# A hybrid decoder layer on one core: rotary row swap by small transfers, attention scores on 64 rows per map, and three convolution taps per channel group on TensorE

## The chip, the cores and the metric

The kernel runs on one core of one Trainium2 chip. The metric is the device time of one execution in microseconds (us), the median over runs. Engines are named as in the profile: PE is TensorE (matmuls; PEld are its weight loads), DVE is VectorE, ACT is ScalarE, POOL is GpSimd, SP is the engine whose queue issues most transfers.

## The reference, cut to what matters

One layer over 512 positions of width 1024. After an RMS norm one projection feeds two groups: a causal depthwise convolution with 31 taps over 512 channels, and differential attention with 4 heads, each with two softmax maps of head size 64. Their outputs are joined, projected back and added. Then follow an expert retrieval over 16384 single-neuron experts, and a gated embedding. The change touches only the first two groups:

```python
def rope(x, pos):                      # x: ..., 64 values per map
    ...
    x1, x2 = x[..., :half], x[..., half:]
    return jnp.concatenate([x1 * cos - x2 * sin, x2 * cos + x1 * sin], axis=-1)

def diff_attention(q, k, v, lam, subln_g, lambda_init):
    qf = rope(q.astype(jnp.float32), pos) * (d ** -0.5)
    kf = rope(k.astype(jnp.float32), pos)
    ...                                # per block of 128 queries:
        s = jnp.einsum('bhcqd,bhckd->bhcqk', qblk, kf)      # c: the two maps
        s = jnp.where(mask, s, -jnp.inf)
        pr = jax.nn.softmax(s, axis=-1)
        a = pr[:, :, 0] - lam * pr[:, :, 1]
        return jnp.einsum('bhqk,bhkd->bhqd', a, vf)
    ...

def conv_module(cv, cg, w, b, ln_g, ln_b):
    u = cv * jax.nn.sigmoid(cg)
    y = lax.conv_general_dilated(u, w[:, None, :], (1,), [(CONV_KERNEL - 1, 0)], ...) + b   # one filter per channel
    return jax.nn.silu(layer_norm(y, ln_g, ln_b))
```

## The kernel before, in words

Channels lie on the 128 partitions and the 512 positions along the free dimension in the whole front part. A projection tile (`proj`, line 144) is 128 output channels by 512 positions: the weight tile is loaded (512 KB), split into a high and a low part in a rounded float type (`split`, line 62: ACT makes the high part, DVE the low one), and multiplied in three products for each of 8 slices of the contraction, 24 matmuls in all (`mm3`, line 66, so lines 67 to 69 in the profile). Plain f32 matmuls, such as the scores, appear in the trace as two matmul instructions each.

The order of the front part in the program is: the eight projections of the convolution (loop at line 182: gate, value, product `u`), the value projections of the attention (line 216), then `qk(h)` for heads 0 and 1, and the loop at line 332, which runs over the 16 units (head, block of 128 queries). In it `att_scores` (line 248) computes the two maps of a unit, adds the causal mask by one more matmul (`identb`, `maskb`), takes the negated maximum on DVE and the exponential on ACT. `att_mix` follows two units later, `att_value` three, and `qk(h + 2)` stands behind the last unit of head `h`. Embedding products (`embed`, line 321) fill the middle. `sub_norm` and `head_out` finish a head; for all but the last head the inverse square root runs on POOL and DVE waits for it. Then come the loading and splitting of the eight tiles of the output weight (line 355), the convolution's taps (line 363), its layer norm (line 369), and the output projection (`outp`, line 402).

That is the program's order only. A planner writes each engine's queue: it takes the instructions by priority as their inputs become ready in its own estimate, and the order so found is fixed. So the taps, which stand behind the attention in the program, run on DVE from the moment `u` exists, in whatever places are free. Each engine then works its queue strictly in that order and waits where an input is late. SP's queue of transfers is such a queue too.

`qk(h)` rotates q and k: the 128 rows of a tile are two maps of 64, and the rotation needs row p next to row p XOR 32. Before, that swap is a matmul with a permutation matrix (`perm`, lines 232 and 233), of which DVE reads the result from PSUM (line 235). DVE then multiplies the rows by cos (line 236, in place) and adds. For k the sum goes into `kr` (line 238). For q it goes into `qz` (line 242), which holds each map in its own copy, with the other map's 64 rows zero; POOL writes these zeros at the start (lines 155 to 157). The scores (line 253) therefore contract 128 rows, of which 64 are zero.

The convolution keeps its output in `cy`: ACT writes the first tap and the bias (line 364), and DVE adds the other 30 taps of each of the four channel groups, one instruction of 128x512 each (line 366).

Of the kernel before, what the change touches and what calls it, by code (L numbers as in the profile page):

```python
# [10 lines left out]
F32 = mybir.dt.float32  # L11
# [5 lines left out]
AF = mybir.ActivationFunctionType  # L17
OP = mybir.AluOpType
# [3 lines left out]
S, D = 512, 1024  # L22
NT = S // 128
KT = D // 128
H, HD = 4, 64
TAPS = 31
NH, NK, TOPK = 8, 128, 16
HC = 2 * NH
NA = 3
# [25 lines left out]
def hymba_layer(ctx: ExitStack, tc: tile.TileContext, I, out):  # L55
    nc = tc.nc
    V, A, P, T = nc.vector, nc.scalar, nc.gpsimd, nc.tensor

    def load(dst, src):
        nc.sync.dma_start(dst, src)  # L60
# [28 lines left out]
    def cload(name, shape, src, pool=None):  # L89
        t = (pool or att).tile(shape, F32, name=name)  # L90
        load(t, src)
        return t
# [4 lines left out]
    def bank():  # L97
        return psf.tile([128, 512], F32, name="bank")

    def bank2():  # L100
        return psf.tile([128, 512], F32, name="bank2", bufs=2)
# [4 lines left out]
    cy = mid.tile([128, 4, S], F32, name="cy")  # L106
    att = tc.alloc_tile_pool(name="att", bufs=1, side="right")
    inp = tc.alloc_tile_pool(name="inp", bufs=1)
# [35 lines left out]
    def proj(i, w=None):  # L144
        hi, lo = w or weight(I["w_in"][i], [128, KT, 128])
        ps = bank()
        for k in range(KT):
            mm3(ps, hi[:, k], lo[:, k], aH[:, k], aL[:, k], k == 0, k == KT - 1)
        return ps

    PADW = TAPS - 1
    u = mid.tile([128, 4, PADW + S], F32, name="u")
    V.memset(u[:, :, 0:PADW], 0.0)
    qz = att.tile([128, H, 2, S], F32, name="qz")
    for h in range(H):
        P.memset(qz[64:128, h, 0], 0.0)
        P.memset(qz[0:64, h, 1], 0.0)
    kr = att.tile([128, H, S], F32, name="kr")
    vn = att.tile([128, NT, S], F32, name="vn")
    pgs = proj(12 + 4, (hi0, lo0))  # L160
    ident = cload("ident", [128, 128], I["ident"], const)
    iota = cload("iota", [128, 128], I["iota"].to_broadcast([128, 128]), const)
    convw = cload("convw", [128, 4, TAPS], I["convw"], mid)
    convb = cload("convb", [128, 4], I["convb"], mid)
# [12 lines left out]
    for t in range(NT):  # L177
        rb = inp.tile([128, 128], F32, name="rb", bufs=2)
        A.activation(rb, ones, AF.Copy, scale=rn[:, t:t + 1])
        T.matmul(rp[:, t * 128:t * 128 + 128], rb, ident, start=True, stop=True)  # L180
    A.activation(r1, rp, AF.Copy)
    for ct in range(4):
        pg = pgs if ct == 0 else proj(12 + 4 + ct)
        sg = inp.tile([128, S], F32, name="sg", bufs=2)
        V.tensor_tensor(sg, pg, r1, op=OP.mult)
        A.activation(sg, sg, AF.Sigmoid)
        pv = proj(12 + ct)
        cvr = inp.tile([128, S], F32, name="cvr", bufs=2)
        V.tensor_tensor(cvr, pv, r1, op=OP.mult)
        V.tensor_tensor(u[:, ct, PADW:], cvr, sg, op=OP.mult)  # L190

    perm = cload("perm", [128, 128], I["perm"])
    cos = cload("cos", [128, S], I["cos"])
    sin = cload("sin", [128, S], I["sin"])
    cmask = cload("cmask", [128, 128], I["cmask"])
# [4 lines left out]
    maskb = att.tile([128, 128], BF16, name="maskb")  # L200
    identb = att.tile([128, 128], BF16, name="identb")
# [15 lines left out]
    for k2 in range(KT // 2):  # L217
        hi, lo = weight(I["w_v"][k2], [128, 2, S])
        for j in range(2):
            k = 2 * k2 + j  # L220
            for t in range(NT):
                sl = slice(t * 128, t * 128 + 128)
# [4 lines left out]
    def qk(h):  # L227
        for isk in range(2):
            ps = proj(4 * isk + h)
            raw = inp.tile([128, S], F32, name="qraw", bufs=2)  # L230
            A.activation(raw, ps, AF.Copy, scale=1.0 if isk else HD ** -0.5)
            pp = bank2()
            T.matmul(pp, perm, raw, start=True, stop=True)
            rot = inp.tile([128, S], F32, name="rot", bufs=2)
            V.tensor_tensor(rot, pp, sin, op=OP.mult)
            V.tensor_tensor(raw, raw, cos, op=OP.mult)
            if isk:
                V.tensor_tensor(kr[:, h], raw, rot, op=OP.add)
            else:
                for c in range(2):  # L240
                    sl = slice(c * HD, c * HD + HD)
                    V.tensor_tensor(qz[sl, h, c], raw[sl], rot[sl], op=OP.add)


    zz = att.tile([128, H, NT, 5], F32, name="zz")
# [1 line left out]

    def att_scores(h, t):
        W = (t + 1) * 128
        pr = []  # L250
        for c in range(2):
            ps = bank()
            T.matmul(ps[:, :W], qz[:, h, c, t * 128:W], kr[:, h, :W], start=True, stop=False)
            T.matmul(ps[:, t * 128:W], identb, maskb, start=False, stop=True)
            nm = att.tile([128, 1], F32, name="nm", bufs=8)
            V.tensor_reduce(nm, ps[:, :W], axis=AX.X, op=OP.max, negate=True)
            p = att.tile([128, S], F32, name="p%d" % c, bufs=MIX + 2)
            A.activation(p[:, :W], ps[:, :W], AF.Exp, bias=nm, accum_out=zz[:, h, t, c:c + 1])
            pr.append(p)
        un[h, t] = pr  # L260
# [67 lines left out]

    units = [(h, t) for h in range(H) for t in range(NT)]
    qk(0)  # L330
    qk(1)
    for i in range(len(units) + MIX + 1):
        if i < len(units):
            h, t = units[i]
            att_scores(h, t)
            if t == NT - 1 and h + 2 < H:
                qk(h + 2)
        if 0 <= i - MIX < len(units):
            att_mix(*units[i - MIX])
        if 0 <= i - MIX - 1:  # L340
            h, t = units[i - MIX - 1]
            att_value(h, t)
            if t == 2 and h > 0:
                head_out(h - 1)
        if i == EMB:
            embed_load()
        if 0 <= i - EMB - 1 < 2 * NT:
            embed(*divmod(i - EMB - 1, 2))
# [6 lines left out]
    for k in range(KT):  # L355
        raw = wop.tile([128, D], F32, name="woraw", bufs=2)
# [4 lines left out]


    for ct in range(4):
        A.activation(cy[:, ct], u[:, ct, 0:S], AF.Identity, scale=convw[:, ct, 0:1], bias=convb[:, ct:ct + 1])
        for j in range(1, TAPS):
            V.scalar_tensor_tensor(cy[:, ct], u[:, ct, j:j + S], convw[:, ct, j:j + 1], cy[:, ct], op0=OP.mult, op1=OP.add)


# [28 lines left out]
    op = tc.alloc_tile_pool(name="op", bufs=2, reuse_waits="tile")  # L397
# [71 lines left out]
    def rbank():  # L469
        return psr.tile([128, 512], F32, name="rbank")  # L470
# [170 lines left out]
    for h in range(NH):  # L641
        for c in range(2):
            raw = wqp.tile([128, KT, 128], F32, name="qraw", bufs=3)
# [5 lines left out]
            ps = rbank()  # L649
# [157 lines left out]
    for c in range(NK):  # L807
# [25 lines left out]
        if NU <= c < NU + 2 * KT and (c - NU) % 2 == 0:  # L833
            k = (c - NU) // 2
            raw = tw.tile([128, D], F32, name="et")
# [45 lines left out]
def _arrays(a):  # L881
# [9 lines left out]
        "subg": c(a["subln_g"][0][:, None]),  # L891
        "convw": c(a["conv_w"][0].T.reshape(4, 128, TAPS).transpose(1, 0, 2)),
        "convb": c(a["conv_b"][0].reshape(4, 128).T),
# [41 lines left out]
```

## Time and profile before

| | |
|---|---|
| median of 3 runs | 1573.29 us (1571.17 to 1575.72) |
| profiled execution | 1571.18 us, of which the span from first to last instruction is 1569.4 us |
| PE, DVE, ACT, POOL busy over the span | 96%, 80%, 46%, 30% |
| granted TensorE clock, mean over the span | 0.987 of full speed |

The shares over the whole span are a mean over stages with different limits. From about 300 us on the kernel streams the experts' weights through TensorE, with DMA busy; the front part, which is changed, is the first 250 us. In the rows, a time at the head of a line is the start in us from the start of the span, and the number behind it is the time from the start of the first to the end of the last instruction that the line merges; "x4" is their number. In brackets stands how long the engine was idle before it and who ended that. TensorE's matmuls overlap, so the distance between two starts, not the duration, tells what a matmul takes in a stream.

### The profile page before, as it was taken

The numbers are of one execution on the slowest core, as the hardware profiler recorded it, in microseconds if no ns is written. First come the engines' busy times: TensorE is split into PE (matmuls) and PEld (weight loads), VectorE is DVE, ScalarE is ACT, GpSimd is POOL, SyncE is SP. The second block draws the span as 40 slices with busy tenths as digits, with TensorE's granted clock in tenths as the row PEclk, the third lists the DMA queues.
The fourth block names the chain that finished last, engine by engine and source line by source line (L and its number), as shares of the span: only waits on it lengthen the run. The fifth ranks groups of instructions, "written<-read, shape, count | busy, mean of one in ns | idle before, by whom it ended". The sixth has DMA issues, their size and how long they took to land. (4 is left out here: it accounts for less than half of the span.)

```text
span 1569.4 us, 22408 instructions
## 1 busy us (share of the span) xinstructions
PE 1512.0 (96%) x7945; PEld 1319.3 (84%) x7945; DVE 1250.5 (80%) x2415; ACT 720.7 (46%) x1133; POOL 469.6 (30%) x324
## 2 busy tenths in 40 slices
PE   8999898999999999999999999999999999998997
PEld 6867566889999988999999888888888888886886
DVE  4999863799999999988885578878778787768756
ACT  5433664223347755776666433333333333234433
POOL 1000103331223344344443234444344443432000
PEclk9999998999999999999999999999999999999999
DMA  7220245311779999999999998899999898989712
GB/s 240 94 81 28 74 161 211 104 59 41 255 213 332 333 340 332 345 388 392 356 360 370 334 369 322 325 338 335 336 330 334 301 327 304 323 327 327 243 40 81
DMA packets 147296, 408.27 MB, mean 260 GB/s; under 512 B 14576, under 2 KB 65776, under 8 KB 145648
## 3 DMA queue, kind: packets, MB, share of 16 engines
q1 hardware_dynamic: 109744, 270.51, 48.9%
q0 software_dynamic: 36864, 134.23, 22.7%
q10 hardware_dynamic: 576, 2.10, 0.3%
q8 instruction: 62, 1.02, 0.3%
q14 instruction: 50, 0.41, 0.1%
HBM read 355.48 MB, written 51.31 MB: 259 GB/s over the span
## 5 line engine op out<-in xcount | busy, mean ns | idle before, releaser
L582 POOL DMA_INDIRECT row<-in_v,bidx x128 | 213.1, 1665 | 299.5 <-DVE acc L593 283.0
L582 POOL DMA_INDIRECT row<-in_u,bidx x128 | 194.6, 1521 | 349.2 <-DVE row L585 304.5
L69 PE MATMUL ups<-mTH,ulo 128*128 128x384 f32 x760 | 256.9, 338 | 3.7 <-DVE ulo L607 3.6
L67 PE MATMUL ups<-mTH,uhi 128*128 128x384 f32 x760 | 258.0, 339 | 0.0
L68 PE MATMUL ups<-mTL,uhi 128*128 128x384 f32 x760 | 256.3, 337 | 0.0
L746 PE MATMUL y<-vlo,hH 128*128 128x512 f32 x768 | 239.4, 393 | 7.0 <-DVE vlo L64 7.0
L746 PE MATMUL y<-vhi,hH 128*128 128x512 f32 x768 | 238.7, 392 | 3.6 <-ACT vhi L63 3.6
L606 ACT ACTIVATE uhi<-uraw 128x1024 fp32r<-128x1024 f32 x128 | 135.2, 1060 | 229.7 <-PE ups L68 157.4
L746 PE MATMUL y<-vhi,hL 128*128 128x512 f32 x768 | 238.4, 392 | 0.0
L63 ACT ACTIVATE hH<-hf 128x384 fp32r<-128x384 f32 x128 | 67.2, 525 | 298.9 <-PE y L746 227.4
L607 DVE TENSOR_TENSOR ulo<-uraw,uhi 128x1024 fp32r<-128x1024 f32 x124 | 150.4, 1218 | 46.6 <-ACT uhi L606 43.3
L746 PEld LDWEIGHTS y<-vlo,hH 128*128 128x128 f32 x768 | 144.8, 189 | 40.1 <-DVE vlo L64 9.7
L746 PEld LDWEIGHTS y<-vhi,hH 128*128 128x128 f32 x768 | 144.3, 189 | 33.7 <-ACT vhi L63 5.1
L585 DVE SCALAR_TENSOR_TENSOR row<-row,mB 128x1024 f32<-128x1024 f32 x128 | 152.3, 1221 | 25.2 <-DMA row<-in_u,bidx 25.1
L746 PEld LDWEIGHTS y<-vhi,hL 128*128 128x128 f32 x768 | 145.4, 189 | 30.6
L593 DVE SCALAR_TENSOR_TENSOR acc<-row,bh,acc 128x1024 f32<-128x1024 f32 x127 | 162.3, 1278 | 0.0
L64 DVE TENSOR_TENSOR hL<-hf,hH 128x384 fp32r<-128x384 f32 x128 | 71.2, 556 | 113.9 <-ACT hH L63 113.9
L64 DVE TENSOR_TENSOR vlo<-vraw,vhi 128x1024 fp32r<-128x1024 f32 x128 | 156.0, 1219 | 3.4 <-ACT vhi L63 3.2
L69 PEld LDWEIGHTS ups<-mTH,ulo 128*128 128x128 f32 x760 | 142.6, 188 | 5.4 <-DVE ulo L607 5.3
L67 PEld LDWEIGHTS ups<-mTH,uhi 128*128 128x128 f32 x760 | 142.7, 188 | 1.1 <-ACT av L613 0.3
L68 PEld LDWEIGHTS ups<-mTL,uhi 128*128 128x128 f32 x760 | 142.7, 188 | 1.0
L63 ACT ACTIVATE vhi<-vraw 128x1024 fp32r<-128x1024 f32 x128 | 135.6, 1059 | 8.7 <-DMA vraw<-in_v 8.4
(280 smaller groups left out, 2629.1 us busy)
## 6 DMA issues: line engine op xcount, KB each, us to landing
uraw<-in_ut SPq DMA_DIRECT2D x128, 512.0 KB, 6.3
vraw<-in_v SPq DMA_DIRECT2D x128, 512.0 KB, 5.0
g_spill<-stage SPq DMA_DIRECT2D x12, 2048.0 KB, 10.2
gt<-g_spill SPq DMA_DIRECT2D x16, 1536.0 KB, 11.3
a_spill<-av SPq DMA_DIRECT2D x101, 192.0 KB, 6.7
ga<-a_spill SPq DMA_DIRECT2D x101, 192.0 KB, 6.4
qraw<-in_wq SPq DMA_DIRECT2D x16, 512.0 KB, 3.6
wraw<-in_w_in SPq DMA_DIRECT2D x15, 512.0 KB, 3.7
```

The costliest lines, as they stand in the source:

```text
L63: A.activation(hi, src, AF.Copy)
L64: V.tensor_tensor(lo, src, f32(hi), op=OP.subtract)
L67: T.matmul(ps, wh, xh, start=first, stop=False)
L68: T.matmul(ps, wh, xl, start=False, stop=False)
L69: T.matmul(ps, wl, xh, start=False, stop=last)
L582: P.indirect_dma_start(out=row, out_offset=None, in_=I["u"] if i < 128 else I["v"], in_offset=bass.IndirectOffsetOnAxis(ap=bidx[:, j:j + 1 ...
L585: tc.keep_in_program_order(V.scalar_tensor_tensor(row, row, 1.0, mB, op0=OP.mult, op1=OP.mult, accum_out=ba[:, j:j + 1]))
L593: tc.keep_in_program_order(V.scalar_tensor_tensor(acc, row, bh[:, j:j + 1], acc, op0=OP.mult, op1=OP.add))
L606: A.activation(hi, raw, AF.Copy)
L607: (P if c in first[:POOLED] else V).tensor_tensor(lo, raw, f32(hi), op=OP.subtract)
L746: T.matmul(y[t][n], w[:, sl], x[:, n * 512:n * 512 + 512], start=c == 0 and w is hH and x is hi, stop=c == NK - 1 and l)
```

## The change

It has three parts. The rotary swap becomes four transfers of 32 rows from the tile `raw` to a new tile `swap`, on SP's queue; the product with cos, which overwrites `raw`, comes after them. q is kept once (`qr`, 128 rows with both maps), one addition each for q and k, and each map's scores contract its own 64 rows; both maps' scores are issued before the two mask matmuls. And the first three taps of each channel group are matmuls of `u` with a diagonal matrix that ACT makes from `ident`, summed in PSUM, from where ACT writes them with the bias to `cy`; DVE adds the other 28.

```diff
+PTAPS = 3
...
-    qz = att.tile([128, H, 2, S], F32, name="qz")
-    for h in range(H):
-        P.memset(qz[64:128, h, 0], 0.0)
-        P.memset(qz[0:64, h, 1], 0.0)
+    qr = att.tile([128, H, S], F32, name="qr")
...
+    def first_taps(ct):
+        ps = bank()
+        for j in range(PTAPS):
+            dg = inp.tile([128, 128], F32, name="rb", bufs=2)
+            A.activation(dg, ident, AF.Copy, scale=convw[:, ct, j:j + 1])
+            T.matmul(ps, dg, u[:, ct, j:j + S], start=j == 0, stop=j == PTAPS - 1)
+        A.activation(cy[:, ct], ps, AF.Identity, bias=convb[:, ct:ct + 1])
+
     for ct in range(4):
...
         V.tensor_tensor(u[:, ct, PADW:], cvr, sg, op=OP.mult)
-
-    perm = cload("perm", [128, 128], I["perm"])
+        if ct:
+            first_taps(ct - 1)
+    first_taps(3)
+
...
-            pp = bank2()
-            T.matmul(pp, perm, raw, start=True, stop=True)
+            swap = inp.tile([128, S], F32, name="swap", bufs=2)
+            for p in range(0, 128, 32):
+                load(swap[p:p + 32], raw[p ^ 32:(p ^ 32) + 32])
+            V.tensor_tensor(raw, raw, cos, op=OP.mult)
             rot = inp.tile([128, S], F32, name="rot", bufs=2)
-            V.tensor_tensor(rot, pp, sin, op=OP.mult)
-            V.tensor_tensor(raw, raw, cos, op=OP.mult)
-            if isk:
-                V.tensor_tensor(kr[:, h], raw, rot, op=OP.add)
-            else:
-                for c in range(2):
-                    sl = slice(c * HD, c * HD + HD)
-                    V.tensor_tensor(qz[sl, h, c], raw[sl], rot[sl], op=OP.add)
+            V.tensor_tensor(rot, swap, sin, op=OP.mult)
+            V.tensor_tensor((kr if isk else qr)[:, h], raw, rot, op=OP.add)
...
-        pr = []
+        pr, sc = [], [bank(), bank()]
         for c in range(2):
-            ps = bank()
-            T.matmul(ps[:, :W], qz[:, h, c, t * 128:W], kr[:, h, :W], start=True, stop=False)
-            T.matmul(ps[:, t * 128:W], identb, maskb, start=False, stop=True)
+            hd_ = slice(c * HD, c * HD + HD)
+            T.matmul(sc[c][:, :W], qr[hd_, h, t * 128:W], kr[hd_, h, :W], start=True, stop=False)
+        for c in range(2):
+            T.matmul(sc[c][:, t * 128:W], identb, maskb, start=False, stop=True)
+        for c, ps in enumerate(sc):
...
     for ct in range(4):
-        A.activation(cy[:, ct], u[:, ct, 0:S], AF.Identity, scale=convw[:, ct, 0:1], bias=convb[:, ct:ct + 1])
-        for j in range(1, TAPS):
+        for j in range(PTAPS, TAPS):
             V.scalar_tensor_tensor(cy[:, ct], u[:, ct, j:j + S], convw[:, ct, j:j + 1], cy[:, ct], op0=OP.mult, op1=OP.add)
```

## Rows read from the trace of the kernel before

**Rows 1.** Windows: length, busy us of each engine (instructions), clock, DMA share, GB/s.
```profile
40.00:106.15 66.15, 66.15 (x287) 53.25 (x286) 65.86 (x97) 25.16 (x31) 0.00 (x0) 1.00 0.29 96
106.15:183.40 77.25, 70.81 (x325) 47.42 (x324) 72.24 (x159) 39.07 (x122) 6.28 (x24) 0.98 0.11 38
183.40:200.20 16.80, 12.37 (x56) 6.74 (x54) 12.35 (x24) 10.89 (x31) 2.74 (x12) 1.00 0.33 109
200.20:249.50 49.30, 48.23 (x201) 37.33 (x202) 28.92 (x39) 24.87 (x42) 0.00 (x0) 1.00 0.53 184
```
The engines stand in the order PE, PEld, DVE, ACT, POOL.

**Rows 2.** Windows, instructions of line 366 alone (taps, DVE).
```profile
40.00:106.15 66.15, 39.05 (x57) 1.00 0.29 96
106.15:183.40 77.25, 36.95 (x52) 0.98 0.11 38
183.40:200.20 16.80, 8.88 (x12) 1.00 0.33 109
sum 160.20, DVE 84.88; mean DVE 28.29
```

**Rows 3.** Timeline of PE: embedding products, then a unit's scores at 512 columns.
```profile
162.33 1.88 PE L324 MATMUL bank<-wraw 128*128 128x512 f32 x4
164.05 1.02 PE L253 MATMUL bank<-kr,qz 128*128 128x512 f32 x2
...
164.96 1.08 PE L253 MATMUL bank<-kr,qz 128*128 128x512 f32 x2
165.88 0.22 PE L254 MATMUL bank<-maskb,identb 128*128 128x128 bf16 x1
```

**Rows 4.** Timeline of all engines around the first rotation.
```profile
87.83 0.58 ACT L231 ACTIVATE qraw<-bank 128x512 f32<-128x512 f32 x1
...
88.25 0.39 PE L67 MATMUL bank<-aH,whi 128*128 128x512 f32 x1
...
88.48 1.11 PE L233 MATMUL bank<-qraw,perm 128*128 128x512 f32 x2
...
89.66 0.39 PE L69 MATMUL bank<-aH,wlo 128*128 128x512 f32 x1
...
89.73 0.68 DVE L235 TENSOR_TENSOR rot<-bank,sin 128x512 f32<-128x512 f32 x1
```

**Rows 5.** Timeline of SP: one issue of a small load.
```profile
34.41 0.43 SPq L60 DMA_DIRECT2D clnb<-in_clnb  x1
```

**Rows 6.** DMA issues: KB each, median us from issue to landing.
```profile
e_spill<-cvr SPq DMA_DIRECT2D x8, 256.0 KB, 2.0
...
ident<-in_ident SPq DMA_DIRECT2D x1, 64.0 KB, 3.8
```

**Rows 7.** Groups by line and shape, 0 to 290 us: busy us, mean ns, idle before.
```profile
L242 DVE TENSOR_TENSOR qz<-qraw,rot 64x512 f32<-64x512 f32 x8 | 5.5, 682 | 0.1
```

**Rows 8.** Timeline of PE behind the first three units of scores.
```profile
113.59 0.44 PE L271 MATMUL bank<-ident,p 128*128 128x128 f32 x1 [3.18 <-DVE p L268]
113.83 1.92 PE L253 MATMUL bank<-kr,qz 128*128 128x512 f32 x2
```

**Rows 9.** Windows, PE alone: length, busy (instructions), granted clock, DMA share, GB/s.
```profile
114.00:116.00 2.00, 2.00 (x5) 0.50 0.00 0
```

**Rows 10.** Waits of DVE from 110 to 200 us: total, times, longest.
```profile
DVE rsq L298 <- POOL rsq L84: 6.7, 3, 2.3
```

**Rows 11.** Timeline of DVE, end of the attention.
```profile
188.74 0.75 DVE L366 SCALAR_TENSOR_TENSOR cy<-u,convw,cy 128x512 f32<-128x512 f32 x1
...
194.60 3.10 DVE L366 SCALAR_TENSOR_TENSOR cy<-u,convw,cy 128x512 f32<-128x512 f32 x4
197.62 0.17 DVE L297 RECIPROCAL of<-of 128x4 f32<-128x4 f32 x1
```

**Rows 12.** Timeline of PE: mean and variance of the convolution's layer norm.
```profile
197.76 1.13 PE L371 MATMUL bank<-cy,ones 128*128 128x512 f32 x2 [1.41 <-DVE cy L366]
...
204.76 1.88 PE L379 MATMUL bank<-csq,ones 128*128 128x512 f32 x4
```

**Rows 13.** Instructions on the tile woraw: ns min/median/max, first and last start.
```profile
L63 ACT ACTIVATE woH<-woraw x8: 1041/1060/1084, 199.0 to 222.5; 128x1024 fp32r<-128x1024 f32 x8
```

## The prediction

> **What bounds the kernel now.** I read the stages first [rows 1]: one row per stretch, with each engine's busy time. From 40 to 106 us TensorE is busy for all 66.15 us and VectorE for 65.86: two engines are full at once. From 106 to 183 (scores, softmax and values of the four heads) TensorE has 70.81 of 77.25 and VectorE 72.24. From 183 to 200 neither is full (12.37 and 12.35 of 16.80): there the latency of the last head's chain counts. From 200 to 249 (output projection) TensorE is full again, 48.23 of 49.30. Then the taps in the first three of these stretches [rows 2]: VectorE runs 57 of the 120 convolution taps before the scores, 52 beside them and 12 in the last stretch (one lies on a border and counts twice), so they fill VectorE up to the end. What moves the end of this front part moves the whole kernel, since all that follows needs the output projection. Behind it no line is changed, so I carry the shift of the front through unchanged.
>
> **The change, part by part.**
>
> *Taps on TensorE.* Added: 4 groups x 3 = 12 plain f32 matmuls over 512 columns. Their price: four instructions, which are two f32 matmuls, fill 162.33 to 164.05, so 0.86 us each [rows 3]; 12 x 0.86 = 10.3. They fall between 42 and about 70 us, where TensorE has no idle time [rows 1], so all of it is on the path: +10.3. ScalarE makes 12 small diagonals; even at the 0.58 us of a whole 128x512 copy [rows 4] this is 7 us, and ScalarE is idle for 41 of these 66 us [rows 1]: nothing. If that cover failed, the 7 us would be the price.
>
> *Row swap.* Removed: eight f32 matmuls by the permutation. One stands between projection steps that otherwise start 0.23 us apart (88.25, 88.48): 88.48 to 89.66 holds it and one more step, so 1.18 - 0.23 = 0.95 us [rows 4]. Three of the eight (q0, k0, q1) run before the scores: -2.9. Five run beside them: -4.8. In their place stand 32 transfers on SP's queue. Behind them there wait the next weights; three buffers hold these ahead, two projections of 24 x 0.23 = 5.5 us, so they are not urgent. The swapped rows come later than the matmul's did: before, the copy starts at 87.83 and the product with sin at 89.73, 1.3 us behind its end [rows 4]. Now SP needs 0.43 us for an issue [rows 5], 1.7 for four, and landing takes between 2.0 (a 256 KB store) and 3.8 us (a 64 KB load) [rows 6]; together 3.7 to 5.5 us. Both products wait for that, since `raw *= cos` overwrites what the transfers read, and behind them on VectorE wait the maxima, the mixes and the weight splits. But the planner that wrote the queue's order has dozens of taps to put in front, and k1 is used only after a whole further pair of projections, 11 us. I take 0. Bounds: 0, and 8 x (5.5 - 1.3) = 34 us of VectorE's time if the products stand where they stand now.
>
> *Taps and zero halves off VectorE.* Two of 30 taps a group go: 8 at 84.88 / 120 = 0.71 us [rows 2] are 5.7 us. The two half-height additions of q become one: 4 x 0.68 = 2.7 us [rows 7]. Together 8.4 us. Before 106 us this moves no end, because TensorE sets the pace there. But the front gets 10.3 - 2.9 = 7.4 us longer, in which VectorE does ten more taps. So of the 64 taps that stand beside and behind the scores now, 8 are gone and 10 are done: 46 remain, and the 12 of the last stretch fall away. The eight zero fills on POOL at the start keep nobody waiting: 0.
>
> *What that gives back.* (a) Where the scores start, TensorE waits 3.18 us for the first mixed map from VectorE [rows 8], and then the granted clock falls to 0.50, the 1.2 GHz level [rows 9]: the pair of f32 instructions at 113.83 took 1.92 us, the pair at 164.05 took 1.02, and the next pair lost somewhat less: 1.5 lost in all, with the wait 4.7. In that gap VectorE also runs k1's three rotation steps of 0.68 [rows 4], which now come behind it. I take -3 (bounds 0 and -4.7). (b) VectorE's three waits for POOL's square root, 6.7 us [rows 10], stay, and so do the TensorE gaps behind them: 0. (c) In the last stretch a tap of 0.75 us sits in the last mix's steps, and a run of taps ends only where the last reciprocal starts, 197.62 [rows 11]; TensorE waits 1.41 us for the last tap [rows 12]. With the taps gone from there: -2.1 (bounds 0 and -3.5). (d) The layer norm's last mean and its four variance matmuls run after 197.7, mostly in the full stretch [rows 12]: 5 x 0.86 = 4.3 us of TensorE. With earlier taps they can go into the idle 4.4 us before 200. But the eight output weights come in a chain of load and split from 199.0 to 222.5 [rows 13], so TensorE may only trade this for waits. I take -2 (bounds 0 and -4.3).
>
> *Scores on 64 rows.* Same columns, same two passes per f32 matmul; at 512 columns map 0 takes 0.91 and map 1 0.92 us, each with its mask matmul [rows 3]. With 128 to 512 columns (2.5 times the largest) that is 4.5 us a head, 18 in all. No row of before shows a 64-row matmul. Bounds: -9, if the two maps run wholly beside each other, and +5, if each of the 32 changes between 64 and 128 rows shows the tail that a matmul otherwise hides under the next one (0.39 long at a pitch of 0.23 [rows 4], so 0.16). I take -2: passes start in order, so only the second pass of map 0 can lie beside the first of map 1, a quarter of 18 (-4.5), and for each change I set the 0.09 by which a perm in the stream costs more than a bare f32 matmul (0.95 - 0.86), 32 x 0.09 = +2.9.
>
> The Trainium skill, TensorEngine Tiling (Array Packing), section Tiling Modes, says that row tiles work independently and can execute in parallel, but also that a change of the tiling mode drains the engine. No run so far shows either; the first would give about the -9 end, the second is the rule behind rival 4.
>
> Sum: +7.4 - 4.8 - 3 - 2.1 - 2 - 2 = -6.5 us. The profiled execution took 1571.2 (span 1569.4 and 1.8 around it), 2.1 below the median 1573.3 of the three runs. So 1564.7 for such an execution, 1567 for the median. Less than 0.3% (4.7 us) can't be told from no change here.
>
> **Rivals.**
> 1. *TensorE pays and gets nothing back.* The gaps and the last stretch stay because they come from latency and from POOL, not from taps; scores as before: +7.4 - 4.8 = +2.6, so 1576. For it: VectorE's only waits are for POOL [rows 10]. Against: the tap in the last mix and the wait for the last tap [rows 11, 12].
> 2. *The swapped rows come late at the head of VectorE's queue* (slower). If the products are placed as if the rows were there after some 2 us, each stalls VectorE for 2 to 3.5 us. Five of eight lie beside the scores: 5 x 3 = 15 us, against the 5 that VectorE has free there [rows 1] and the 12.7 of the 18 taps fewer. The give-backs (a), (c), (d), 7.1, are then lost, the scores gain nothing (+2), and stalls in front of maxima reach TensorE for some 3: -6.5 + 7.1 + 2 + 3 = +5.6, so 1579. It decides from about 3 us of stall at each product. Against: there are taps enough to put in front.
> 3. *Both maps side by side*: scores -9 instead of -2, total -13.5, so 1560. For it: the operands lie in separate halves. Against: the passes' order.
> 4. *Changes of shape drain TensorE*: +5.1 in place of -2, total +0.6, so 1574. For it: every score unit has two changes. Against: the mask matmuls, another type, break the stream already and add 0.05.
>
> **Chances.** Forecast 45%, its own range 1562 to 1571; four fifths of it are faster by over 0.3%. Rival 1 20%, nearly all within. Rival 2 14%, most of it slower. Rival 3 9%, faster. Rival 4 12%, within. Faster 0.45, within 0.38, slower 0.17. Range 1557 to 1580: all four rivals lie inside by their own price; the far bound of the swap is left out as unlikely.
>
> **What would show it.** Right: the first scores start near 113.5 us instead of 106.15; TensorE's wait behind them is under 2 us, with no stretch at 0.50; the last taps end before the last mix; map 1's first pass lies under map 0's second; the output projection ends near 243 instead of 249.5. Wrong: VectorE idles over 10 us in all before the products with cos and sin (rival 2); TensorE keeps its gaps (rival 1); the scores at 512 columns take over 1.83 us a unit (rival 4). A difference that arises behind the output projection, where no line changed, would make the whole sum wrong.

## The result and the profile after

The changed kernel takes 1582.09 us (median of 9 runs, 1578.45 to 1585.84), the kernel before 1573.29 in as many runs beside it: ratio 1.0063, 95% interval 1.0050 to 1.0076. It is slower by 9 to 10 us; forecast was 1567, 6.5 us faster, with a range of 1557 to 1580. The profiled execution took 1582.05 us, 10.9 more than that of before.

Windows of the kernel after, with the columns of [rows 1]: up to the first scores, scores to the last score, the last stretch, the output projection.

```profile
40.00:122.30 82.30, 78.90 (x312) 59.51 (x312) 76.95 (x111) 28.82 (x43) 0.00 (x0) 0.95 0.26 81
122.30:194.20 71.90, 62.37 (x312) 40.66 (x313) 63.89 (x142) 38.62 (x122) 5.15 (x24) 0.95 0.22 66
194.20:212.10 17.90, 14.29 (x60) 8.68 (x56) 6.26 (x16) 11.85 (x33) 2.37 (x12) 0.90 0.32 103
212.10:262.60 50.50, 49.85 (x201) 38.17 (x202) 27.07 (x36) 24.32 (x41) 0.00 (x0) 0.97 0.53 180
```

Against the four lengths of [rows 1] (66.15, 77.25, 16.80, 49.30) that is +16.15, -5.35, +1.1 and +1.2, together 13.1 us; 2.4 of them are won back behind the output projection, where no line changed (1317.5 us instead of 1319.9; over twelve of the kernels here this part takes 1313.8 to 1320.2, so 2.4 is within its scatter), and 10.7 of span remain. The forecast had +7.4, -9.8, -2.1 and -2.0. So every stage came out above its forecast: by 8.75, 4.45, 3.2 and 3.2. VectorE, on the other hand, lost its work as forecast: it is busy for 63.89 us of the scores' stage and 6.26 of the last stretch, where it had 72.24 and 12.35. That this bought so little is the main finding below.

The taps on VectorE, windows of their line alone (answers to [rows 2]):

```profile
40.00:122.34 82.34, 52.46 (x77) 0.95 0.26 81
122.34:192.00 69.66, 25.65 (x36) 0.95 0.23 67
192.00:212.00 20.00, 0.00 (x0) 0.91 0.29 95
```

The last stretch holds no taps, as forecast, and it is still 1.1 us longer.

TensorE's timeline at the first diagonal taps, and at the second group of them:

```profile
38.36 1.09 PE L178 MATMUL bank<-ident,rb 128*128 128x128 f32 x4 [0.52 <-ACT rb L177]
43.10 5.49 PE L185 MATMUL bank<-u,rb 128*128 128x512 f32 x6 [3.64 <-DVE u L196]
47.60 1.39 PE L68 MATMUL bank<-aH,whi 128*128 128x512 f32 x1
...
59.53 2.74 PE L185 MATMUL bank<-u,rb 128*128 128x512 f32 x6
```

and the clock there, a window with the columns of [rows 1]:

```profile
43.00:49.00 6.00, 5.90 (x8) 2.71 (x9) 2.77 (x7) 2.46 (x5) 0.00 (x0) 0.51 0.00 1
```

The first group stands at the head of TensorE's queue and waits 3.64 us for `u`, with the ready products of the next projection behind it. Then it runs at a granted clock of 0.51, the 1.2 GHz level, and takes 5.49 us where the same six instructions take 2.74 sixteen microseconds later. The clock had fallen ahead of this wait: from 38.7 to 39.4 us it is 0.50. In the kernel before those products filled this place (24 start from 36 to 43 us, here one), at 1.00.

TensorE at the start of the scores (answers to [rows 8] and, with the window, to [rows 9]):

```profile
122.34 0.49 PE L257 MATMUL bank<-kr,qr 64*128 64x128 f32 x4
...
130.17 0.45 PE L277 MATMUL bank<-ident,p 128*128 128x128 f32 x1 [5.17 <-DVE p L274]
130.54 2.08 PE L257 MATMUL bank<-kr,qr 64*128 64x512 f32 x4
```
```profile
130.40:133.00 2.60, 2.60 (x8) 0.95 (x8) 2.60 (x9) 0.28 (x1) 0.00 (x0) 0.50 0.38 139
```

The wait that was to go, 3.18 us, is now 5.17, and the half clock is there as before. The wait is what is left of a chain across the engines when TensorE has done its own work. The end of that work (third unit's masks) after and before, with the first score of before:

```profile
124.71 0.28 PE L259 MATMUL bank<-maskb,identb 128*128 128x128 bf16 x2
```
```profile
106.15 0.38 PE L253 MATMUL bank<-kr,qz 128*128 128x128 f32 x2
...
110.19 0.22 PE L254 MATMUL bank<-maskb,identb 128*128 128x128 bf16 x1
```

From the first score to the first transposed map the chain takes 7.83 us (122.34 to 130.17), before 7.44 (106.15 to 113.59 [rows 8]). TensorE's own work in it fell from 4.26 us to 2.65, since the scores are shorter and the permutation of k1 is gone. So of the 2.0 us by which the wait grew, 1.6 are work that TensorE lost, and 0.4 a map that comes later. VectorE's timeline just ahead shows why the map comes no earlier:

```profile
123.30 0.29 DVE L262 TENSOR_REDUCE nm<-bank 128x1 f32<-128x128 f32 x1
123.50 0.69 DVE L243 TENSOR_TENSOR qraw<-qraw,cos 128x512 f32<-128x512 f32 x1
124.10 0.69 DVE L245 TENSOR_TENSOR rot<-swap,sin 128x512 f32<-128x512 f32 x1
...
127.16 1.21 DVE L65 TENSOR_TENSOR wlo<-wraw,whi 128x1024 fp32r<-128x1024 f32 x1
...
128.47 0.69 DVE L243 TENSOR_TENSOR qraw<-qraw,cos 128x512 f32<-128x512 f32 x1
129.07 0.69 DVE L245 TENSOR_TENSOR rot<-swap,sin 128x512 f32<-128x512 f32 x1
129.67 0.35 DVE L274 SCALAR_TENSOR_TENSOR p<-p,zz,p 128x128 f32<-128x128 f32 x1
```

Between the first maximum and the first mixed map (129.67) lie five of the six rotation steps of q1 and k1 and a weight split. Before, k1's three lay there, a weight split (107.38) and a tap (112.08).

One unit of scores at 512 columns (answers to [rows 3]):

```profile
176.36 1.13 PE L257 MATMUL bank<-kr,qr 64*128 64x512 f32 x4
177.42 0.29 PE L259 MATMUL bank<-maskb,identb 128*128 128x128 bf16 x2
```

The four instructions of both maps take 1.06 us up to the mask, where one map of 128 rows took 0.86 (164.05 to 164.91, the start of its mask): both maps run side by side, and what is left over is 0.2 us. At 384, 256 and 128 columns it is 0.85, 0.63 and 0.43 for both. Both masks included, up to the next matmul, the four units of a head took 0.61, 1.03, 1.46 and 1.88 us before, together 5.0 (the prediction had 4.5); now they take 0.54, 0.75, 0.97 and 1.18, together 3.4. That is some 6 us less over four heads.

The end of VectorE's part (answers to [rows 11]):

```profile
195.00 0.69 DVE L262 TENSOR_REDUCE nm<-bank 128x1 f32<-128x512 f32 x1 [0.17 <-PE bank L259]
198.21 0.17 DVE L304 TENSOR_TENSOR rsq<-rsq,zz 128x4 f32<-128x4 f32 x1 [2.52 <-POOL rsq L85]
198.29 0.68 DVE L262 TENSOR_REDUCE nm<-bank 128x1 f32<-128x512 f32 x1
200.31 0.17 DVE L272 RECIPROCAL zz<-zz 128x2 f32<-128x2 f32 x1 [1.34 <-ACT p L264]
...
205.06 0.75 DVE L314 SCALAR_TENSOR_TENSOR cL<-bank,subg,cH 128x512 fp32r<-128x512 f32 x1 [3.49 <-ACT cH L313]
209.18 0.18 DVE L303 RECIPROCAL of<-of 128x4 f32<-128x4 f32 x1 [3.36 <-ACT of L302]
```

Where the taps lay, VectorE now waits: 2.52 us for POOL, then 1.34, 3.49 and 3.36 for ScalarE. The second maximum of the last unit has even got behind the wait for POOL. TensorE does the whole mean in the last stretch, as before (193.6 to 198.9), and the eight instructions of the variance still stand in the output projection (answers to [rows 12]):

```profile
205.81 3.62 PE L376 MATMUL bank<-cy,ones 128*128 128x512 f32 x8
...
212.09 2.04 PE L68 MATMUL bank<-woH,cH 128*128 128x512 f32 x5 [0.62 <-ACT woH L64]
...
214.80 4.36 PE L384 MATMUL bank<-csq,ones 128*128 128x512 f32 x8
```

And yet the taps' absence shortened the last unit's chain; TensorE's clock took it back. The run `late_fewer` (below) has the same instructions in the same order on TensorE there. First the transposes of the last mixed map, of the changed kernel and of `late_fewer`, then the window of the last stretch of `late_fewer`:

```profile
201.72 0.63 PE L277 MATMUL bank<-ident,p 128*128 128x128 f32 x4 [2.05 <-DVE p L274]
```
```profile
189.88 0.63 PE L278 MATMUL bank<-ident,p 128*128 128x128 f32 x4 [2.04 <-DVE p L275]
```
```profile
182.40:199.50 17.10, 13.50 (x61) 7.82 (x58) 7.15 (x17) 12.68 (x33) 2.37 (x12) 0.98 0.33 107
```

Both waited equally long, 2.05 and 2.04 us. Over the next 4.3 us the granted clock is 0.60 in the changed kernel (201.7 to 206.0) and 1.00 in `late_fewer`. From the last mask to the first product of the output projection it is 17.36 us (194.73 to 212.09) and 15.71 (182.89 to 198.60); in the kernel before it was 16.73 (183.44 to 200.17), at 1.00. So at full clock the chain is 1.0 us shorter without the taps, and the half clock costs 1.65. Why the clock fell in one of the two and not in the other is not shown.

### The profile page after: what moved, and what is told of

It reads as the page before. It is cut to its first block, busy times and chain, and to the rows that moved or that the text cites. A ratio compares the mean times of both kernels' runs of the same rounds, so it can differ in the third digit from the quotient of the medians.

```text
span 1580.1 us, 22481 instructions
## 1 busy us (share of the span) xinstructions
PE 1515.8 (96%) x7953; PEld 1318.2 (83%) x7953; DVE 1244.6 (79%) x2403; ACT 724.0 (46%) x1145; POOL 463.5 (29%) x316
```

## The experiments

Each ratio is to the kernel before in runs on the same chip; 0.1% are 1.6 us. The intervals are some 0.13% to either side, so a difference of two ratios is uncertain by about 3 us. `no_taps`, `swap_only` and `half_only` leave out parts of the change; `no_swap`, `no_half` and `taps_only` undo parts. Two numbers return: the taps' own time on TensorE (10.3 us) and the price of their place (3.6 us of wait and some 2.9 at half clock).

**The parts, one by one.** Without the diagonal taps (`no_taps`, the first tap back on ScalarE):

```diff
-        if ct:
-            first_taps(ct - 1)
-    first_taps(3)
...
-        for j in range(PTAPS, TAPS):
+        for j in range(1, TAPS):
```

> Row swap by transfers and scores on 64 rows, but all taps on VectorE as before. Theory A: the changed kernel less 10.3 us of taps and 6.5 us of wait and half clock, plus some 6 us because VectorE is full again beside the scores: about 1571 (1568 to 1575). Rival B: less 10.3 alone, plus 6: 1578. Rival C: the swap's price stays: about 1580, and the wait behind the first scores stays at 5 us.

Measured: 1567.98 us, ratio 0.9977 (0.9965 to 0.9989). This is the lower end of theory A's range; rivals B and C are out, although the wait behind the first scores that rival C named is there (6.1 us). The taps are 0.86%, 13.5 us, of the changed kernel's time.

With the permutation matmul in place of the transfers (`no_swap`):

```diff
-            swap = inp.tile([128, S], F32, name="swap", bufs=2)
...
+            T.matmul(pp, perm, raw, start=True, stop=True)
```

> Taps on TensorE and scores on 64 rows, but the rows swapped by the permutation matmul as before. Theory A: eight matmuls of 0.95 us come back, 7.7 us, and the wait behind the first scores falls from 5.2 to about 3 us with the clock's fall after it: +4 to +6, about 1587. Rival C: the late swapped rows cost more than the matmuls: 1576 or less.

Measured: 1583.9, ratio 1.0089 (1.0073 to 1.0104), so 4.1 us over the changed kernel: the lower end of theory A's 4 to 6. Rival C is out.

With 128-row scores and zero halves (`no_half`; the swapped rows share buffers with the gates):

```diff
+            T.matmul(ps[:, :W], qz[:, h, c, t * 128:W], kr[:, h, :W], start=True, stop=False)
```

> Taps on TensorE and row swap by transfers, but scores on 128 rows with zero halves and two additions for q (the swapped rows use a tile slot of the convolution's gate, which is free by then). Theory D (two maps run side by side and save 6.4 us of TensorE, which shows in the end): about 1588 to 1590. Rival E (the scores' time is hidden by the softmax's latency on VectorE and ScalarE): 1582 to 1584.

Measured: 1586.52, ratio 1.0102 (1.0084 to 1.0120), so 6.1 us over the changed kernel. That is theory D's 6.4 within the intervals, and not rival E.

The taps alone (`taps_only`: both edits above together), and the 64-row scores alone on the kernel before (`half_only`):

> The kernel before with the three tap matmuls alone. Theory A' (the taps cost what they cost in the changed kernel, 14 us between it and the version without them, whatever the scores and the swap do): 1586 (1584 to 1588) where before is 1572. Rival C (the taps lose only together with the late swapped rows): 1580 or less.

Measured: 1588.67, ratio 1.0110 (1.0090 to 1.0130): a little over the range of theory A'. The taps lose without the other two parts as well.

> The kernel before with the 64-row scores alone (rows swapped by the matmul, all taps on VectorE). Theory D (side by side, some 6 us of TensorE and 2.7 us of VectorE less, of which 4.4 showed in the changed kernel): 1567 to 1569 where before is 1572. Rival E (hidden behind the softmax): 1571 to 1573.

Measured: 1575.24, ratio 1.0023 (1.0010 to 1.0036). 64-row scores by themselves are a loss of 3.6 us, which neither theory had. TensorE's busy time beside the scores fell, and the time went into waits and half clock at the scores' start; window and timeline of `half_only`:

```profile
105.60:184.70 79.10, 68.70 (x322) 43.25 (x323) 72.41 (x157) 38.21 (x122) 5.95 (x24) 0.94 0.11 37
```
```profile
113.55 0.45 PE L266 MATMUL bank<-ident,p 128*128 128x128 f32 x1 [4.14 <-DVE p L263]
```

TensorE idles 10.4 us of this stage, against 6.4 [rows 1], its clock is 0.94 instead of 0.98, and the stage is 1.9 us longer. The last stretch, with a clock of 0.91 instead of 1.00, is 1.5 us longer too (18.30).

The transfers alone (`swap_only`, in the kernel before; the swapped rows share buffers with the gates here too):

```diff
-            T.matmul(pp, perm, raw, start=True, stop=True)
...
+                load(swap[p:p + 32], raw[p ^ 32:(p ^ 32) + 32])
```

> The row swap by transfers alone: eight permutation matmuls leave TensorE, scores contract 128 rows with zeroed halves, and all taps are on VectorE. Theory A (eight permutations are worth what they take on TensorE, three ahead of the scores and five beside them, 7.7 us): 1565 to 1568 us. Rival C (the swapped rows come late at the head of VectorE's queue, and the scores wait): 1572 us or more.

Measured: 1568.68, ratio 0.9985 (0.9972 to 0.9998): a gain, but hardly a third of theory A's 7.7 us by ratio. TensorE waits 5.9 us behind the first scores there, again more than 3.18. Late rows don't show: VectorE's waits from 40 to 210 us of that run name POOL, ScalarE and TensorE, none a swap.

**Is side by side worth its rows?** `apart` puts each mask directly behind its map's score:

```diff
             T.matmul(sc[c][:, :W], qr[hd_, h, t * 128:W], kr[hd_, h, :W], start=True, stop=False)
-        for c in range(2):
             T.matmul(sc[c][:, t * 128:W], identb, maskb, start=False, stop=True)
```

> The changed kernel with the mask's matmul directly behind each map's score, so that the two 64-row scores are not neighbours on TensorE and cannot run side by side. Theory D (side by side is worth what TensorE's rows show, 6.4 us over four heads' units): 1585 to 1588 us. Rival E (it is hidden behind the chain score, maximum, exponential, transpose): about 1582 us.

Measured: 1590.06, ratio 1.0116 (1.0101 to 1.0131), 8.3 us over the changed kernel. TensorE's timeline of `apart`:

```profile
203.81 1.12 PE L257 MATMUL bank<-kr,qr 64*128 64x512 f32 x2
204.86 0.23 PE L258 MATMUL bank<-maskb,identb 128*128 128x128 bf16 x1
205.02 1.12 PE L257 MATMUL bank<-kr,qr 64*128 64x512 f32 x2
```

One map of 64 rows by itself takes 1.05 us up to its mask, no less than the two together in the changed kernel. With its mask it takes 1.21 us; with 128 rows it took 0.91 to 0.92 [rows 3]. The 0.30 is the same at 384 columns (1.01 against 0.70, 177.43 to 178.13) and at 128 (0.58 against 0.28), so it belongs to the two changes of height around each map: 0.2 ahead of the mask (1.05 instead of 0.86) and 0.1 behind it (0.16 instead of 0.05). Rival 4's mechanism is real at about the size that the forecast had as its bound, 0.16; side by side a unit has two such changes instead of four, and the rest is more than paid for. The unit grows from 1.18 us with both masks to 2.33 (203.81 to 206.14), sixteen units from some 14 to 27, and TensorE is busy for 78.32 instead of 62.37 us in the stage, part of it at half clock (0.90 there); only about half of these 16 us reach the end. The mechanism of theory D is shown, its 6.4 us was too little because the added changes of height weren't in it.

**The place of the taps.** `late_taps` issues the diagonals of the first two channel groups one projection pair later; the last two groups stay where they were, behind the last pair:

```diff
-        if ct:
-            first_taps(ct - 1)
+        if ct > 1:
+            first_taps(ct - 2)
+    first_taps(2)
```

> The whole change, but each group's three tap matmuls stand one projection pair later in the program, so that TensorE has a projection in front of the first group instead of waiting for u. Theory A (the loss is the place: 3.6 us of wait at the head of TensorE's queue and then some 2.9 us at the half clock): 6.5 us less than the changed kernel, about 1575.5. Rival B (the loss is the taps' own 10.3 us on a full TensorE, and the wait is covered by the 6 us that TensorE has to spare later): no more than 2 us less, 1580 to 1582. Rival C (the loss is the swapped rows that come late where the scores begin): no difference, 1582.

Measured: 1582.05, ratio 1.0070 (1.0058 to 1.0083): no gain, so not theory A as it stands. Yet the wait for `u` is gone, and the scores start at 116.9 instead of 122.3; the 5.4 us were lost again behind. Windows of `late_taps`:

```profile
40.00:116.90 76.90, 76.69 (x311) 58.59 (x310) 71.88 (x106) 29.76 (x44) 0.00 (x0) 0.98 0.29 87
116.90:195.30 78.40, 64.83 (x314) 42.92 (x313) 69.09 (x151) 38.70 (x122) 5.83 (x24) 0.93 0.21 60
```

VectorE has 69.09 us of work beside the scores now, 5.2 more than in the changed kernel: the taps that did not fit before. Whether these eat the gain is asked by leaving work out. `fewer_taps` leaves out the last 14 taps of each group on VectorE (56 of 112, so the convolution is incomplete), `late_fewer` does so with the later diagonals:

```diff
-        for j in range(PTAPS, TAPS):
+        for j in range(PTAPS, TAPS - 14):
```

> The changed kernel without the last 14 taps of each group on VectorE: 56 of 112 taps are left out, so the convolution is not computed in full. In the changed kernel 36 taps (25.65 us) run beside the scores. Theory F (the length of the scores' stage is VectorE's work in it): the stage falls from 71.9 us to TensorE's 62 to 65, the total to 1573 (1571 to 1576). Rival G (the order of the queues and the latency of the softmax set it; taps only fill waits): the stage stays within 3 us and the total at 1579 to 1583.

Measured: 1576.90, ratio 1.0031 (1.0016 to 1.0045), between the ranges of theory F and rival G. No tap is left beside the scores, and the stage goes from 71.9 to 67.9 us only:

```profile
123.50:191.40 67.90, 62.92 (x312) 42.22 (x313) 41.86 (x106) 37.87 (x122) 5.43 (x24) 0.95 0.23 70
```

56 taps, 41.9 us of VectorE's time, are worth 5.2 us: 0.09 us each. So 41.86 us of VectorE and 62.92 of TensorE make a stage of 67.9 without any taps: what is left is TensorE's work and its waits for the chain from score to mix. With fewer taps ahead of them the swapped rows do come late, the mechanism of rival 2. VectorE's waits in `fewer_taps` (total, times, longest):

```profile
DVE qraw L243 <- DMA swap<-qraw: 14.9, 4, 5.7
```

Two of the four lie beside the scores (3.19 and 5.69 us). Whether they cost the kernel time is not shown; the 0.09 us are what a tap is worth with these waits in its place.

> Diagonal taps one projection pair later, and the last 14 VectorE taps of each channel group left out (56 of 112 taps of the convolution on VectorE, so the convolution is incomplete). Theory F' (with the taps later, VectorE's taps beside the scores ate the 5.4 us that the front had gained): with them gone the front's gain comes through, 1576.9 - 5.4 = about 1571.5 us. Rival G' (the scores' stage is set by queue order and latency, not by VectorE's amount of work, and the front's gain is lost there again): about 1577 us.

Measured: 1569.81, ratio 0.9987 (0.9975 to 0.9999), 0.44% or 6.9 us under `fewer_taps`, as theory F' had it. With VectorE relieved the later place pays its whole price back (3.6 + 2.9 was the estimate): the taps beside the scores had eaten it. It also says that a VectorE tap has no fixed price: beside the later diagonals the same 56 are worth 13.1 us (1.0070 to 0.9987), 0.23 us each instead of 0.09.

**Taps in the scores' gaps.** If TensorE idles for some 5 us at the scores' start, taps there should be cheap. `gap_taps` issues the diagonals behind the units 2, 6 and 10, counted from 0; ScalarE starts each group with the fourth tap:

```diff
+GAP = {2: (0, 1), 6: (2,), 10: (3,)}
...
+        part = inp.tile([128, S], F32, name="sg", bufs=2)
+        A.activation(part, ps, AF.Copy)
+        V.tensor_tensor(cy[:, ct], cy[:, ct], part, op=OP.add)
...
+            for ct in GAP.get(i, ()):
+                first_taps(ct)
```

> Swap and 64-row scores, and the tap matmuls put beside the scores, where TensorE waits: two groups behind the third unit's scores, the others behind the seventh's and the eleventh's; ScalarE starts each group with the fourth tap, and VectorE adds the matmuls' sum (27 taps and one addition a group). Theory A'' (three taps on TensorE lose because the stretch ahead of the scores has no room, not in themselves): scores start near 103.5, the wait of 6.1 us and the half clock behind the first scores go, total 1562 to 1566. Rival B (TensorE pays the 10.3 us anywhere): 1572 or more. Rival H (only traded against VectorE's addition): 1567 to 1569, as without taps.

Measured: 1613.79, ratio 1.0265 (1.0241 to 1.0289), for a reason that no theory had. The addition of TensorE's part stands ahead of all of VectorE's taps of its group, so VectorE could not run ahead of the scores:

```profile
40.00:103.00 63.00, 63.00 (x274) 52.16 (x273) 26.06 (x36) 26.79 (x34) 0.00 (x0) 0.97 0.32 100
```
```profile
PE bank L379 <- DVE cy L374: 24.5, 3, 18.3
```

VectorE is busy for 26.06 of the first 63 us (65.86 of 66.15 before [rows 1]), and at the layer norm TensorE waits 24.5 us for the convolution (total, times, longest). `gap_taps2` and `gap_taps3` put part of VectorE's taps, 44 and 60, ahead of these additions:

```diff
+SPLIT = (25, 18, 10, 7)        # gap_taps3: (31, 24, 14, 7)
...
+    for ct in range(4):
+        for j in range(PTAPS + 1, SPLIT[ct]):
+            V.scalar_tensor_tensor(cy[:, ct], u[:, ct, j:j + S], ...)
```

> The 12 diagonal matmuls of the taps are issued between the scores of later heads (one or two channel groups behind a head), and part of VectorE's own taps of each group stands ahead of the addition that needs TensorE's part, so that VectorE can run its taps before the scores start. Theory A'' (the place of the taps sets their price): scores start near 103.5 us as without taps on TensorE, the wait of 6.1 us behind the first scores and the half clock that follows it are filled by the taps, total 1562 to 1566 us. Rival B (TensorE pays its 10.3 us wherever the taps stand): 1572 us or more. Rival H (half is filled, half is paid): 1567 to 1569 us.

Measured: 1576.50, ratio 1.0026 (1.0014 to 1.0039). TensorE's waits behind the first scores are down to 0.64 and 0.18 us, but VectorE ran out of work early (54.84 of 64.3 us) and its last tap starts at 204.3, in the last stretch:

```profile
40.00:104.30 64.30, 64.30 (x284) 52.95 (x283) 54.84 (x81) 26.31 (x34) 0.00 (x0) 1.00 0.34 104
104.30:182.50 78.20, 72.68 (x336) 45.69 (x337) 71.78 (x155) 43.32 (x134) 5.54 (x24) 0.98 0.20 60
182.50:206.30 23.80, 16.93 (x65) 10.45 (x62) 19.58 (x35) 13.66 (x35) 2.88 (x12) 0.80 0.35 113
```

> As the run before with the taps beside the scores, but VectorE is given 60 instead of 44 of its own taps ahead of the additions that wait for TensorE's part, so that it is not left idle in front of the scores (there it was busy for 54.8 of 64.3 us, against 63.4 of 63.5 without taps on TensorE). Theory A'' (in the gaps the taps cost TensorE little; what that run lost at the end, +3.9 us in the last stretch, came from VectorE's idle time): 1576.5 - 4 = 1572 us or less. Rival B (TensorE pays its 10.3 us wherever they stand): 1576 us or more, again.

Measured: 1573.18, ratio 0.9999 (0.9987 to 1.0010). Relieved of that, the same 12 matmuls cost 0.22% or 3.5 us over `no_taps`, where they cost 13.5 in the changed kernel. Place decides, as theory A'' had it, and rival B's 1576 or more is out; but the price does not go all the way to nothing, and theory A'' missed its 1562 to 1566 for `gap_taps2` and, by 1 us, its 1572 or less here.

**What eight taps give back.** `eight_out` is `no_taps` with taps 1 and 2 of each group left out, so VectorE has the changed kernel's 112 taps and TensorE pays nothing for it:

```diff
-        for j in range(1, TAPS):
+        for j in range(3, TAPS):
```

> Swap by transfers and 64-row scores, no taps on TensorE, and two of VectorE's 30 taps in each channel group left out (8 of 120, so the convolution is incomplete): VectorE is left with the 112 taps of the changed kernel, and TensorE pays nothing for it. It measures by itself what eight taps fewer on VectorE give back. By the prediction's steps (a), (c) and (d) the gaps at the scores' start, in the last stretch and in the output projection shrink, by about 7 us: 1561 us. Rival (a tap on VectorE is worth what the run without 56 of them showed, 5.2 us / 56 = 0.09 us each): 8 x 0.09 = 0.7, 1567 us, no different from the 1568.0 without this cut.

Measured: 1568.57, ratio 0.9967 (0.9953 to 0.9981), so 0.10% or 1.6 us under `no_taps` by the ratios, with intervals that overlap. It is not the 7 us of the steps (a), (c) and (d), though taps are still left in its last stretch (4.69 us from 181 to 199), so (c) is tested only in part. The wait behind the first scores is as long as without the cut: TensorE's waits of `eight_out` (total, times, longest):

```profile
PE bank L266 <- DVE zz L261: 8.0, 3, 6.1
```

## Why the prediction was wrong

Its sum had three blocks, and the runs price each (ratios times 1573).

| step | forecast | measured | from |
|---|---|---|---|
| 12 taps on TensorE | +10.3 | +15.1 | changed kernel against `eight_out`: 1.0063 - 0.9967 |
| VectorE relieved: (a), (c), (d) | -7.1 | -1.6 | `eight_out` against `no_taps` |
| eight permutations and 64-row scores | -9.7 | -3.6 | `no_taps` against before |
| sum | -6.5 | +9.9 | 1.0063 |

Each measured difference carries some 3 us. The first two rows can't be parted cleanly: `eight_out` leaves out eight taps, and the ten more that the forecast had VectorE do in the longer front count in the first row. So three steps failed, by 4.8, 5.5 and 6.1 us.

*The give-back, steps (a), (c) and (d).* The prediction took VectorE, full in two stages, for what TensorE waits for, and from every relief of it subtracted a wait. But the wait of 3.18 us [rows 8] is what a chain (maximum, exponential, reciprocal, mix), passing through a queue in a written order, takes beyond TensorE's own work. Freed places in that queue were filled with something else, five rotation steps instead of three, and the chain went from 7.44 to 7.83 us; TensorE's work beside it went from 4.26 to 2.65. So (a) gave nothing: 5.17 us of wait, and the clock at 0.50 as before. In the last stretch the mechanism of (c) was right and its size half of what was forecast: the chain also runs through POOL's root and ScalarE's exponential, squares and root, for which VectorE now waits (2.52, 1.34, 3.49, 3.36), and without the taps it is 1.0 us shorter at full clock instead of 2.1. That the clock could fall in this stretch stood in no term; in the changed kernel's trace it cost 1.65 us. (d) gave nothing, the variance stands where it stood. On the whole this is the first half of rival 1 ("gets nothing back"), which had 20%. A tap of 0.75 us on VectorE was worth 0.09 us in `fewer_taps` and 0.2 in `eight_out` (1.6 / 8).

*The taps' price.* 0.86 us each was right: a group of six instructions takes 2.74 us at full clock. That they fall "where TensorE has no idle time [rows 1], so all of it is on the path" overlooked that a matmul which waits for VectorE closes the place for what stands behind it. Of the 16.15 us of the front, which is counted from 40 us on, 10.3 - 2.9 were forecast; 3.1 are the wait at the head of TensorE's queue (40.0 to 43.1; the rest of its 3.64 lies ahead of 40 us), 2.75 the first group at the lower clock (5.49 - 2.74), 2.3 ten products of 0.23 us that used to run before 40 us and are now held up behind the taps (96 start before 40 us instead of 106), and 0.3 a second wait for `u` (at 76.07). Some 0.3 us are not accounted for. `late_fewer` shows that the place costs this once VectorE is relieved, `gap_taps3` that in a good place TensorE's taps are a third as dear (5.0 us over `eight_out` instead of 15.1).

*The gain on TensorE beside the scores.* The five permutations there were counted at their full 4.8 us, as if TensorE set the pace of that stage. It idles for 6.4 us of it [rows 1], and does so longer when its work shrinks (9.5 us in the changed kernel, 11.9 without the taps). For the 64 rows the forecast took a value between its bounds, -2, where TensorE's rows show some -6. The Trainium skill, TensorEngine Tiling (Array Packing), section Tiling Modes, has row tiles working in parallel and a change of mode drain the engine. The traces agree with both: two maps of 512 columns take 1.06 us where one by itself takes 1.05, and the changes cost 0.2 and 0.1 us. Rival 3's mechanism is what happened on TensorE, without its 1560, since saved time turned into waits. The prediction's reason against it, that passes start in order, was an argument without a row. The parts don't simply add: swap and 64 rows are worth 3.6 us without the taps and 7.4 with them (1.0110 to 1.0063). 64 rows alone lose 3.6 us (`half_only`), beside the swap they give 1.3, less than the intervals can tell (0.9985 to 0.9977), and beside swap and taps 6.1 (1.0102 to 1.0063). Each edit makes the planner write another order, and which wait that order opens was followed only at the scores' start and in the last unit; why 64 rows lose alone and win beside the other two parts stays open.

*What was right:* the swap by transfers. They land after 1.9 to 2.5 us, as the nearer of the two rows said [rows 6], and VectorE never waits for them in the changed kernel, though four issues take 2.41 us where 1.7 was taken from [rows 5]:

```profile
140.53 2.41 SPq L61 DMA_DIRECT2D swap<-qraw  x4
```
```profile
DMA to landing us min/median/max: 1.9/2.0/2.5
```

(The second line is from the view of the tile `swap`.) The reason given, taps enough to put in front, was right as well: with half of the taps gone VectorE waits 14.9 us for swapped rows (`fewer_taps`), and 5.9 us in `gap_taps`. Rival 2's 1579 came nearest to the measured 1582, but its mechanism did not occur in the changed kernel. The small diagonals from ScalarE are not among the waits of TensorE's matmuls in the front, and the taps did leave the last stretch; the zero fills were not tested by themselves. Of the signs named ahead, the scores' start (113.5 forecast, 122.3), the wait under 2 us, no stretch at 0.50, and the projection's end (243 forecast, 262.6) came out wrong, the first three of them in the first 131 us of the trace.

The version without the taps beats both kernels: 0.9977 (0.9965 to 0.9989) of before, 0.9914 of the changed one.

## What to carry to other kernels

A busy share near 100% on two engines at once doesn't make both the bound: ask what one microsecond less on each is worth, and measure it by leaving work out (here 0.09 us for a 0.75 us tap on VectorE, and 0.23 with the diagonals in the later place, against more than its own 0.86 us on TensorE). Work moved between engines is paid at the receiving engine's marginal price, and includes what its wait at the head of an in-order queue holds up and the half clock around it. In a stage paced by a chain across engines, time saved on one of them comes back as idle time until the chain itself gets shorter.

## What the runs showed of the hardware

Two plain f32 matmuls of 64 rows each, in the two halves of the array, run fully side by side if they are neighbours in TensorE's queue: up to the mask the four instructions of 512 columns take 1.06 us in the changed kernel, and two of them alone 1.05 in `apart`. A change from 64 rows to 128 costs about 0.2 us and one back 0.1, whatever the columns (0.30 per map with its mask in `apart`, at 128, 384 and 512). A transfer of 32 rows of 2 KB within the chip's memory lands 2.0 us after its issue and keeps SP's queue for 0.6. And idle time on TensorE can be paid twice: after waits of 3.64 and 5.17 us the granted clock was 0.51 and 0.50 for what followed, which took 5.49 us instead of 2.74, and 2.08 instead of 1.13. The length of the last wait alone does not tell: the clock was 0.50 already ahead of the wait of 3.64 us, and after waits of 2.05, 2.04 and 2.25 us it was 0.60 (changed kernel, 201.7), 1.00 (`late_fewer`, 189.9) and 1.00 (kernel before, 189.6).
